# A hybrid decoder block: the output projection by seven products of quarter matrices

## The chip, the cores and the metric

The kernel runs on one core of one Trainium2 chip. The time is the device time of one execution in microseconds (us), taken as the median of several runs. Beside it stands one execution recorded by the hardware profiler. The engines are named as in the profile: PE (TensorE, matrix multiplies; PEld is its weight load), DVE (VectorE), ACT (ScalarE), POOL (GpSimd) and SP (SyncE, which issues most transfers). "SPq" and "POOLq" are the queues in which an engine issues its transfers.

## The reference

One layer on x of 512 tokens by 1024 channels, all in float32. The normalised input goes through one wide projection, whose columns feed two mixers; their results are merged by two gates, and one more projection closes the layer:

```
h = rms_norm(x, norm_pre)
proj = h @ w_in
...
y_a = (o_a * jax.nn.silu(z_n)) @ w_nsa_o
...
y_b = (o_b * jax.nn.silu(z_r)) @ w_ret_o
merged = jax.nn.sigmoid(m_a) * y_a + jax.nn.sigmoid(m_b) * y_b
x = x + rms_norm(merged @ w_out, norm_post)
```

The change is about the last line: `merged @ w_out`, 512 tokens by 1024 channels times 1024 by 1024, its norm over the 1024 outputs of a token, and the sum with x.

## The kernel before, in words

**Precision.** Every float32 operand is split in a high and a low part (`hi` is a rounded copy, made by ACT or DVE; `lo` is the difference, made by DVE in `sub_split`, lines 242 and 209). Each product is three matmuls: high by high, high by low, low by high (`mm3`, line 237; the matmul itself is line 230).

**Order.** All instructions of all engines are put out by one planner at build time (`Order`, line 45). The stages are Python generators that yield what they wait for: a planned time, an engine, or a flag. The planner adds up planned costs for each engine and always continues the generator that could go on first, so the fixed order of each engine's queue comes out of these estimates. At run time the engines wait on semaphores for the data itself.

**Weights.** `stream` (line 1523) lays out all weights in HBM in the order of use, and `stream_shape` names the pieces. SP loads pieces of 128 x 1024 (512 KB) in four raw buffers (`load_next`, line 349; `NR` is 4). `splitter` (line 374) splits each into two weights of 128 x 512 in a ring of nine pairs (`whi`, `wlo`; `NW` is 9). A pair comes free when the matmuls that use it last are put out (`used_up`).

**Seven products.** Two projections, the second halves of the gates `MA` and `MB`, are already done with seven products of quarter matrices in place of eight (`seven`, line 1219; `product`, line 1199; `seven_end`, line 1232). The weight sums that this takes are made in HBM: `weight_sums` (line 328) has POOL issue four copies from DRAM to DRAM tiles and four accumulating transfers for each, while attention runs, and SP later loads the sums like weights. The sums of the other operand are made by DVE (`h_sum`, line 1173). DVE joins the products in `seven_end`.

**The stages in order** (`PLAN`, line 29): `Z`, `MA`, `ZR`, `QK`, `VR` (retention: `ret`, line 1013), then second halves `ZR`, `QK`, `VR`, then `MB`, `NO`, `RO` of the first 512 channels, `MA` by seven, `NO`, `MB` by seven, `RO` of the second. `NO` and `RO` are the projections to `y_a` and `y_b`; their results come channel by channel (four blocks of 128 channels by 512 tokens, `tra`), and `tail_ya` and `tail_yb` (lines 1304, 1311) multiply them with the gates, add them and split the merged block into `MO_H` and `MO_L` (flag `mg0` to `mg7`).

**The last projection before** (end of `main`): two halves of 512 output columns, each for four blocks of 128 tokens, over eight blocks of 128 channels: 2 x 4 x 8 x 3 = 192 matmuls of 512 columns. The last token block of the second half is put out in two pieces of 256 columns. Each weight of 128 x 512 is used by four token blocks, 12 matmuls. `tail_o` (line 1327) handles each block from PSUM: ACT squares it and sums the squares, DVE adds up and multiplies by `norm_post`, POOL takes the power, DVE scales and adds x, and SP stores. `end_loads` (line 1149) loads x and `norm_post` for it.

**In retention**, `ret` has POOL take one power per token block (`rv`, line 1087); the rest of that block's chain on DVE, PE and ACT waits for it.

Of the kernel before, what the change touches and what calls it, by code (L numbers as in the profile page):

```python
# [18 lines left out]
P = 128  # L19
# [120 lines left out]
def block_kernel(ctx: ExitStack, tc, x, xT, x0s, ws, small, w2s, norm_post, rope_r, dmask, out):  # L140
# [101 lines left out]
    def sub_split(lo, src, hi, r, e="dve"):  # L242
        return tt(lo, src, f(hi), OP.subtract, r, e)
# [67 lines left out]


    loads, off = [], 0
    sums, atts = [], [0]
    mark = sp.tile([P, 1], FT, name="mark")
    for pieces in stream_shape():
        if pieces == "seven":
            b11, b12, b21, b22 = (ws[off + i * P * 1024:off + (i + 1) * P * 1024].rearrange("(p n) -> p n", p=P)
                                  for i in range(4))
            t1, t2, t3, t4 = (dp.tile([P, 1040], FT, name=f"t{len(sums)}{i}")[:, 0:1024] for i in range(4))  # L320
            sums.append(((t1, b11), (t3, b12), (t2, b11), (t4, b21), (t1, b12), (t3, b22), (t2, t3), (t4, t2)))
            loads.extend((a, [1024]) for a in (b11, b21, t2, t3, t1, t4, b22))
# [51 lines left out]
    def splitter():  # L374
        for i, (_, pieces) in enumerate(loads):
            n = sum(pieces)
            for k in range(2):
                p = 2 * i + k
                own = KD <= p < 2 * KD
# [9 lines left out]
                if own:  # L389
# [12 lines left out]
                yield  # L402
# [610 lines left out]
    def ret(hp, t, ps, e):  # L1013
# [134 lines left out]

    def end_loads():
        t = bp.tile([P, 28 * 256], FT, name="ends", tag="low")  # L1150
        XR.extend(t[:, o * 256:o * 256 + D] for o in (0, 4, 24, 0))
        OT.extend([*(t[:, o * 256:o * 256 + D] for o in (8, 12, 16)), at(28, D)])
        XR.append(t[:, 20 * 256:20 * 256 + D])
        for t in range(2):
            DMA.dma_start(XR[t], x[t * P:(t + 1) * P, :])
        DMA.dma_start(XR[2], x[2 * P:3 * P, :])
        DMA.dma_start(XR[4], norm_post.rearrange("(o n) -> o n", o=1).broadcast_to([P, D]))

    shr = [0.0] * 4

    def h_sums():
# [70 lines left out]
    def seven_end(st, n, ps, e):  # L1232
# [3 lines left out]
        if n == 0:  # L1236
# [12 lines left out]
        r = max(e, st["ur"])  # L1249

        def gate_of(i, j, b, r):
            sg = sgw[st["off"] // 4].rearrange("p (f c) -> p f c", f=4)[:, 2 * j:2 * j + 2, i * 256:(i + 1) * 256]
            return sg, tt(sg, v, b.rearrange("p (m c) -> p m c", m=2), OP.add, r)
        sg = None
        if n == 1:
            sg, e = gate_of(0, 0, u, r)
# [20 lines left out]
            return  # L1277
        i, j = at_
        yield e, "dve"
        rv = rsrow[:, i * 256:(i + 1) * 256].unsqueeze(1).broadcast_to([P, 2, 256])  # L1280
        e = stt(sg, sg, -1.0, rv, OP.mult, OP.mult, e) if j else tt(sg, sg, rv, OP.mult, e)
        yield e, "act"
        e = act(sg, sg, AF.Tanh, r=e, scale=0.5)
# [20 lines left out]
    def tail_ya(half, ft, ps, e):  # L1304
        yield od.need(f"sg{half}{ft}")
        yield max(e, sgr[ft]), "dve"
        e = stt(sgs[ft], sgs[ft], 1.0, ps, OP.add, OP.mult, e)
        ACC.put(ps, e)
        od.flags.add(f"ya{half}{ft}")

    def tail_yb(half, ft, ps, e):
        yield od.need(f"ya{half}{ft}", f"sg{half}{4 + ft}")
        yield max(e, sgr[4 + ft]), "dve"
        e = stt(sgs[4 + ft], sgs[4 + ft], 1.0, ps, OP.add, OP.mult, e)
        ACC.put(ps, e)
        e = tt(sgs[ft], sgs[ft], sgs[4 + ft], OP.add, e)
        yield e, "act"
        k = half * 4 + ft
        e = act(MO_H[k], sgs[ft], r=e)
        yield e, "dve"  # L1320
        mor[k] = sub_split(MO_L[k], sgs[ft], MO_H[k], e)
        od.flags.add(f"mg{k}")

    mor = [0.0] * 8
    ss2 = cp.tile([P, NT, 3], FT, name="ss2")

    def tail_o(t, i, c0, n, ps, e):

        hc = slice(c0, c0 + n)
        end = c0 + n == D  # L1330
        sq = yield from NAT.get()
        yield e, "act"
        ea = act(sq[:, :n], ps[:, :n], AF.Square, r=e, scale=1.0 / 32.0, accum_out=ss2[:, t, i:i + 1])
        NAT.put(sq, ea)
        yield ea, "dve"
        if i:
            e = ts(ss2[:, t, i:i + 1], ss2[:, t, i:i + 1], ss2[:, t, i - 1:i], 4e-6 if i == 1 else 0.0,
                   OP.add, OP.add, ea)
        if end:
            r2 = sp.tile([P, 1], FT, name="rr", tag="rr", bufs=4)  # L1340
            er = tt(r2, ss2[:, t, i:i + 1], nhalf[:, 0:1], OP.pow, e, "pool")
        e = tt(OT[t][:, hc], ps[:, :n], XR[4][:, hc], OP.mult, ea)
        ACC.put(ps, e)
# [41 lines left out]
    def main():  # L1385
# [126 lines left out]
def stream_shape():  # L1512

    yield [512, 512]
    yield from [[1024]] * 3
    yield from [[560]] * 4
    yield from [[1024]] * (4 + 8)
    for b in PLAN:
        yield from ["seven"] if b in SEVEN else [[1024]] * (2 if b[0] == "NO" else 4)
    yield from [[1024]] * 8  # L1520


def stream(a):
# [22 lines left out]
    for name, i in PLAN:  # L1546
# [41 lines left out]
```

## Time and profile before

| | us |
|---|---|
| median of the runs | 527.37 (527.1 to 527.5) |
| profiled execution, its own time | 526.86 |
| its span, first to last instruction | 525.1 |
| DVE busy | 404.8 |
| ACT busy | 291.9 |
| POOL busy | 25.9 |
| DMA traffic | 68.87 MB, mean 131 GB/s |

The profiled execution's own time is 1.76 us above its span, and the median of the runs 0.5 us above that. Views used below: the page (busy time of each engine), the chain of waits that ended last, tables of stretches of the span (for each engine its busy time, the number of instructions in brackets, then the granted clock of TensorE, the busy share of the DMA engines and GB/s), timelines of one engine (start, duration, engine, line, what it writes and reads, count, and in brackets the idle time before it), and groups of equal instructions. Consecutive matmuls overlap in these records, so the pace is read from start to start.

### The profile page before, as it was taken

How to read it: one execution, taken by the hardware profiler on the slowest of the kernel's cores; microseconds unless marked ns; L12 is line 12 of the kernel's file. 1: busy time of each engine (PE TensorE's matmuls, PEld its weight loads, DVE VectorE, ACT ScalarE, POOL GpSimd, SP SyncE). 2: the span in 40 equal slices, each digit the busy share in tenths (PEclk: the TensorE clock that was granted, in tenths of full speed). 3: DMA queues.
4: the chain of work that ended last, by engine and by line, in shares of the span. 5: the costliest groups of instructions: out<-in, count | busy, mean ns of one | idle time of the engine just before them, and what ended most of it. 6: DMA issues, size and time to landing. Idle time of an engine off the chain costs nothing.

```text
span 525.1 us, 7867 instructions
## 1 busy us (share of the span) xinstructions
PE 514.8 (98%) x2778; PEld 441.3 (84%) x2778; DVE 404.8 (77%) x980; ACT 291.9 (56%) x630; POOL 25.9 (5%) x56
## 2 busy tenths in 40 slices
PE   9999999999999999999999999999999999999995
PEld 7898888788888888888888888888788989988884
DVE  6798799989979799996876576787889867645533
ACT  6663799768568798763515253524557434323411
POOL 1000000000112011000000000000000000000000
PEclk9999999999999999999999999999999999999998
DMA  8941026501667338433131341131644726624032
GB/s 319 392 166 41 21 81 218 183 2 40 213 230 171 111 70 206 126 121 100 42 120 41 140 138 64 42 121 40 220 141 124 238 81 207 208 108 160 2 109 92
DMA packets 22456, 68.87 MB, mean 131 GB/s; under 512 B 2448, under 2 KB 3728, under 8 KB 22416
## 3 DMA queue, kind: packets, MB, share of 16 engines
q1 hardware_dynamic: 19968, 59.84, 32.8%
q0 software_dynamic: 2304, 8.39, 6.9%
q8 instruction: 22, 0.36, 0.3%
q14 instruction: 18, 0.15, 0.1%
q10 hardware_dynamic: 144, 0.14, 0.1%
HBM read 66.26 MB, written 10.49 MB: 146 GB/s over the span
## 4 chain that ended last, share of the span: by engine, by line
PE 81%; DVE 8%; DMA 5%; issue 2%; ACT 1%; SPq 1%; POOL 0%; POOLq 0%; DVEq 0%; ACTq 0%
PE bank L230 76%; PE bank L234 6%; DVE wlo L209 3%; DMA raw<-in_stream_dram 2%; DMA arena_l<-in_x_dram 2%; DVE arena_r L209 1%; DMA arena_l<-in_xT_dram 1%; DMA arena_f<-in_xT_dram 1%; DVE arena_l L846 1%; ACT arena_l L197 1%; DVE arena_l L218 1%; DVE arena_f L209 1%; SPq L479 0%; DVE nat L209 0%; SPq L356 0%
## 5 line engine op out<-in xcount | busy, mean ns | idle before, releaser
L209 DVE TENSOR_TENSOR wlo<-raw,whi 128x512 fp32r<-128x512 f32 x172 | 112.0, 687 | 6.8 <-ACT whi L197 5.7
L197 ACT ACTIVATE whi<-raw 128x512 fp32r<-128x512 f32 x157 | 94.5, 627 | 40.5 <-PE bank L230 33.5
L230 PE MATMUL bank<-whi,hTh 128*128 128x512 f32 x256 | 100.3, 407 | 0.6 <-DVE arena_r L222 0.5
L230 PE MATMUL bank<-whi,hTl 128*128 128x512 f32 x256 | 96.2, 391 | 0.0
L230 PE MATMUL bank<-wlo,hTh 128*128 128x512 f32 x256 | 96.1, 390 | 0.0
L230 PE MATMUL bank<-arena_r 128*128 128x256 f32 (+2 forms) x328 | 70.9, 336 | 0.3 <-DVE arena_r L209 0.3
L230 PE MATMUL bank<-arena_r,whi 128*128 128x512 f32 (+1 forms) x208 | 63.8, 382 | 1.0 <-DVE sg L222 1.0
L197 ACT ACTIVATE arena_l<-arena_l,stat 128x384 f32<-128x384 f32 (+3 forms) x109 | 57.8, 552 | 4.6 <-DVE stat L209 2.5
L197 ACT ACTIVATE arena_r<-bank 128x512 fp32r<-128x512 f32 (+2 forms) x80 | 45.1, 571 | 23.1 <-PE bank L234 21.5
L230 PEld LDWEIGHTS bank<-whi,hTl 128*128 128x128 f32 x256 | 48.1, 188 | 10.7
L230 PEld LDWEIGHTS bank<-whi,hTh 128*128 128x128 f32 x256 | 48.6, 190 | 9.7 <-DVE arena_r L222 0.9
L230 PEld LDWEIGHTS bank<-arena_r 128*128 128x128 f32 x328 | 51.1, 189 | 6.5 <-DVE arena_r L209 0.6
L209 DVE TENSOR_TENSOR arena_r<-bank,arena_r 128x512 fp32r<-128x512 f32 (+2 forms) x72 | 47.1, 657 | 10.9 <-ACT arena_r L197 10.4
L230 PEld LDWEIGHTS bank<-wlo,hTh 128*128 128x128 f32 x256 | 48.3, 188 | 8.2
L230 PE MATMUL bank<-hTh,whi 128*128 128x512 f32 (+1 forms) x144 | 52.4, 364 | 0.0
L230 PE MATMUL bank<-hTh,wlo 128*128 128x512 f32 (+1 forms) x144 | 51.2, 356 | 0.0
L230 PE MATMUL bank<-hTl,whi 128*128 128x512 f32 (+1 forms) x144 | 51.1, 355 | 0.0
L230 PE MATMUL bank<-whi,arena_r 128*128 128x512 f32 (+1 forms) x176 | 48.6, 352 | 0.0
L230 PEld LDWEIGHTS bank<-arena_r,whi 128*128 128x128 f32 x208 | 38.8, 188 | 8.8 <-DVE sg L222 1.6
L230 PE MATMUL bank<-arena_r,wlo 128*128 128x512 f32 x96 | 37.4, 389 | 0.0
L230 PEld LDWEIGHTS bank<-whi,arena_r 128*128 128x128 f32 x176 | 32.2, 189 | 4.6
L234 PE MATMUL bank<-ident,arena_l 128*128 128x128 f32 (+1 forms) x232 | 33.9, 273 | 0.9 <-DVE arena_l L566 0.9
(165 smaller groups left out, 771.0 us busy)
## 6 DMA issues: line engine op xcount, KB each, us to landing
raw<-in_stream_dram SPq DMA_DIRECT2D x77, 512.0 KB, 4.2
t<-in_stream_dram POOLq DMA_DIRECT2D x12, 512.0 KB, 5.4
raw<-t SPq DMA_DIRECT2D x8, 512.0 KB, 3.7
arena_f<-in_rope_r_dram SPq DMA_DIRECT2D x8, 256.0 KB, 2.6
t<-t POOLq DMA_DIRECT2D x4, 512.0 KB, 5.2
arena_f<-in_xT_dram SPq DMA_DIRECT2D x8, 256.0 KB, 3.7
ends<-in_x_dram SPq DMA_DIRECT2D x4, 512.0 KB, 5.4
arena_l<-in_xT_dram SPq DMA_DIRECT2D x7, 256.0 KB, 5.5
```

The lines of the kernel that those rows point to most:

```text
L197: S.activation(o, i, func, **kw)
L209: (V if e == "dve" else G).tensor_tensor(o, a, b, op=op)
L218: V.tensor_scalar(o, a, s1, s2, op0=op0, op1=op1)
L230: T.matmul(ps, a, b, start=start, stop=stop)
L234: T.transpose(ps, a, idn)
L846: V.tensor_tensor_reduce(pv[:, b, :], sv[:, b, :], maskp[:, 512 - L:512], 1.0, -NEG, OP.add, OP.min, nm[:, b:b + 1])
```

## The change

The last projection is cut in quarters: tokens 0 to 255 and 256 to 511, channels in two halves, output columns in two halves. With merged quarters a (token half, channel half) and weight quarters b (channel half, column half), it takes seven products, each of two blocks of 128 tokens by four blocks of 128 channels by 512 columns.

- **Weights.** `stream` gives four quarters of two pieces each. The four weight sums, of two pieces each, are made by 16 transfers that POOL issues (`out_sums`): eight copies to DRAM tiles, then eight accumulating ones. Three follow the power of each of the first four token blocks in `ret`, and one that of each of the second four (`OSUMS`). SP loads 14 pieces in place of eight. The last eight weights have places of their own, which come free after the second `RO`.
- **Merged sums.** `s_early` makes the sum that needs the first channel half only, `s_late` the three others, on DVE, with splits by ACT and DVE into the places of `hTh` and `hTl`. The gates of the second half go to new places (`G1`), so that the first merged half stays.
- **Products.** `out_seven` runs seven products into PSUM banks `X` (products 1, 3, 5, 7), `Q` (2, 4) and `Y` (6). Where a product's partial value is needed in another sum, ACT copies the bank first (`keep`) and the next product adds to it in PSUM. The last product finishes its first token block before its second.
- **Tails.** `tail_o` takes a kept copy to add (`plus`) for six of eight blocks. Its final scaling is in three pieces for token block 1; the second piece of block 0 is put behind the power of block 1. x comes in two loads with `norm_post` after the gates, and two after the merged sums.

```
+        if pieces == "out":
+            b11, b12, b21, b22 = ([ws[off + i * P * 1024:off + (i + 1) * P * 1024].rearrange("(p n) -> p n", p=P)
+                                   for i in range(2 * q, 2 * q + 2)] for q in range(4))
+            t1, t2, t3, t4 = ([dp.tile([P, 1040], FT, name=f"o{i}{j}")[:, 0:1024] for j in range(2)] for i in range(4))
+            for a, b in ((t1, b11), (t3, b12), (t2, b11), (t4, b21), (t1, b12), (t3, b22), (t2, t3), (t4, t2)):
+                osums.extend(zip(a, b))
+            loads.extend((a, [1024]) for q in (b11, t3, t2, t4, t1, b21, b22) for a in q)
...
+    def out_sums(n):
...
+        for _ in range(n):
+            i = len(oissued)
+            o, a = osums[i]
+            if i < 8:
+                G.dma_start(o, a)
+            else:
+                G.dma_start(o, a, accum_op=OP.add)
+            od.op("pool", 900.0)
+            oissued.append(i)
...
+        out_sums(OSUMS[4 * hp + t])
...
+    def s_early(s):
...
+        yield od.need("end00", "end01", "end10", "end11")
+        t = yield from RS.get()
+        yield 0.0, "dve"
+        e = tt(t, sgs[s][:, 0:256], sgs[s][:, 256:512], OP.subtract)
+        yield e, "act"
+        sor[0][s] = yield from s_split(2 * s + 1, slice(0, 256), t, e)
+        RS.put(t, sor[0][s])
+        od.flags.add(f"se{s}")
...
+    def s_late(s, r):
+        yield r, "dve"
+        m0, m1, t = sgs[s], G1[s], sgs[4 + s]
+        e = tt(t[:, 0:256], m1[:, 256:512], m0[:, 256:512], OP.subtract, r)
+        e = stt(t[:, 256:512], t[:, 0:256], -1.0, m0[:, 0:256], OP.mult, OP.subtract, e)
+        es = e
+        yield e, "act"
+        sor[1][s] = yield from s_split(2 * s, slice(0, 512), t, e)
+        od.flags.add(f"sl{s}")
+        yield 0.0, "act"
+        mor[4 + s] = yield from mo_split(4 + s, m1, 512, r)
+        yield od.need(f"se{s}")
+        yield es, "dve"
+        e = stt(m0[:, 256:512], t[:, 256:512], -1.0, m1[:, 0:256], OP.mult, OP.subtract, es)
+        yield e, "act"
+        s4r[s] = e = yield from s_split(2 * s + 1, slice(256, 512), m0[:, 256:512], e)
+        od.flags.add(f"s4{s}")
+        if all(f"s4{i}" in od.flags for i in range(4)):
...
+    def tail_o(t, i, ps, e, plus=None):
+        hc = slice(i * 512, (i + 1) * 512)
+        o = OT[t][:, hc]
+        if plus:
+            yield lambda: len(plus[0]) > plus[1]
+            b, r = plus[0][plus[1]]
+            yield max(e, r), "dve"
+            e = tt(o, ps, b, OP.add, max(e, r))
+            free[t, i] = e
+            src = o
+        else:
+            src = ps
+        yield e, "act"
+        ea = act(rsrow, src, AF.Square, r=e, scale=1.0 / 32.0, accum_out=ss2[:, t, i:i + 1])
...
+            e = ts(ss2[:, t, 1:2], ss2[:, t, 1:2], ss2[:, t, 0:1], 4e-6, OP.add, OP.add, ea)
...
+            er = tt(r2, ss2[:, t, 1:2], nhalf[:, 0:1], OP.pow, e, "pool")
+            od.flags.add(f"pow{t}")
+        tt(o, src, XR[4][:, hc], OP.mult, ea)
+        if not i:
             return
...
+        if t > 1:
+            yield lambda: len(parts) == 2 * len(loads)
+        for a, b in ((0, 512), (512, D)) if t != 1 else ((0, 384), (384, 768), (768, D)):
+            if t == 0 and a:
+                yield od.need("pow1")
             e = stt(OT[t][:, a:b], OT[t][:, a:b], r2, XR[t][:, a:b], OP.mult, OP.add, e)
             DMA.dma_start(out[t * P:(t + 1) * P, a:b], OT[t][:, a:b])
...
+        plan = ((X, quarter(0, 0)), (Q, summed(2)), (X, summed(1)), (Q, quarter(1, 1)), (X, summed(0)),
+                (Y, quarter(0, 1)), (X, summed(3)))
+        first, last = (0, 1, 5), (3, 5, 6)
+        for n, (ps, (of, src)) in enumerate(plan):
...
+            for ms in ((0, 1),) if n < 6 else ((0,), (1,)):
+                for s in range(4):
+                    name, rd, k = src(s)
+                    yield od.need(name)
+                    yield rd[k] + PE_LAG
+                    yield blk.ready(4 * n + s)
+                    yield blk.ready(4 * n + s)
+                    wh, wl, r = blk.views(4 * n + s)
+                    for m in ms:
+                        lh, ll = of(s, m)
+                        for i, (a, b) in enumerate(((lh, wh), (ll, wh), (lh, wl))):
+                            T.matmul(ps[m], a, b, start=n in first and s + i == 0, stop=n in last and s + i == 5,
+                                     skip_group_check=True)
+                            e = od.pe(228.2, r)
+                    if ms[-1] == 1:
+                        used_up(e)
+                if n == 6:
+                    od.spawn(tail_o(ms[0], 1, ps[ms[0]], e), 1)
+            for m in range(2):
+                if n == 0:
+                    if m == 0:
+                        od.spawn(flip(), 1)
+                    od.spawn(keep(ps[m], p1, e), 1)
+                elif n == 1:
+                    od.spawn(keep(ps[m], p7, e), 1)
+                elif n == 2:
+                    od.spawn(keep(ps[m], u1, e, G1[2 + m]), 1)
+                elif n == 3:
+                    od.spawn(tail_o(2 + m, 0, ps[m], e, (u1, m)), 1)
+                elif n == 4:
+                    od.spawn(tail_o(2 + m, 1, ps[m], e, (p7, m)), 1)
+                elif n == 5:
+                    od.spawn(tail_o(m, 0, ps[m], e, (p1, m)), 1)
+
...
-        for half in range(2):
-            blk = Block(8, 512)
-            for t in range(NT):
-                c = slice(t * P, (t + 1) * P)
-                n = 256 if half and t == NT - 1 else 512
-                for j in range(512 // n):
-                    ps, e = yield from nat(blk, t, n, t == NT - 1 and (j + 1) * n == 512,
-                                           lambda kt: MO_H[kt][:, c], lambda kt: MO_L[kt][:, c], j * n, merged)
-                    od.spawn(tail_o(t, half + j, half * 512 + j * n, n, ps, e), 1)
...
+        od.flags.add("gb")
+        yield from out_seven()
```

More of the change, by code (lines that the diff above doesn't have):

```diff
@@ L40 @@
 HOLD = 1500.0
+OSUMS = (3, 3, 3, 3, 1, 1, 1, 1)
 CAPS = (0, 4, 8, 11, 14, 16, 16, 16, 16)
@@ L302, in block_kernel @@
     XH = Ring([at(o, 512) for o in (28, 38, 40)])
+    G1 = []
     SH, low = [], [arena_l]
@@ L313, in block_kernel @@
     loads, off = [], 0
-    sums, atts = [], [0]
+    sums, osums, oissued, atts = [], [], [], [0]
     mark = sp.tile([P, 1], FT, name="mark")
@@ L378, in splitter @@
                 p = 2 * i + k
-                own = KD <= p < 2 * KD
+                late = p - 2 * len(loads) + 8
+                own = KD <= p < 2 * KD or late >= 0
+                if late >= 0:
+                    yield od.need("gb")
                 yield lambda: own or in_ring(p) < in_ring(len(done)) + NW
@@ L388, in splitter @@
                 src = raws[i][0][:, k * m:(k + 1) * m]
-                if own:
+                if late >= 0:
+                    hi, lo = at(4 * late, 512, FR), at(4 * late + 2, 512, FR)
+                elif own:
                     hi, lo = WC[p - KD]
@@ L1150, in end_loads @@
         t = bp.tile([P, 28 * 256], FT, name="ends", tag="low")
[L1151 to L1154, printed above, removed]
+        v = [t[:, o * 256:o * 256 + D] for o in range(0, 28, 4)]
+        OT.extend(v[0:4])
+        XR.extend([at(30, D), at(34, D), *v[4:7]])
+        DMA.dma_start(XR[4], norm_post.rearrange("(o n) -> o n", o=1).broadcast_to([P, D]))
+        for t in range(2, 4):
             DMA.dma_start(XR[t], x[t * P:(t + 1) * P, :])
-        DMA.dma_start(XR[2], x[2 * P:3 * P, :])
-        DMA.dma_start(XR[4], norm_post.rearrange("(o n) -> o n", o=1).broadcast_to([P, D]))
+            od.dma(P * 4096)
     shr = [0.0] * 4
@@ L1243, in seven_end @@
         yield od.need(*[f"mg{k}" for k in range(4)])
+        if not st["off"]:
+            yield od.need("sh3")
         if n == 3:
@@ L1251, in gate_of @@
         def gate_of(i, j, b, r):
-            sg = sgw[st["off"] // 4].rearrange("p (f c) -> p f c", f=4)[:, 2 * j:2 * j + 2, i * 256:(i + 1) * 256]
-            return sg, tt(sg, v, b.rearrange("p (m c) -> p m c", m=2), OP.add, r)
+            c = slice(i * 256, (i + 1) * 256)
+            bv = b.rearrange("p (m c) -> p m c", m=2)
+            if st["off"]:
+                sg = [(sgw[1].rearrange("p (f c) -> p f c", f=4)[:, 2 * j:2 * j + 2, c], v, bv)]
+            elif j:
+                sg = [(at(38, 1024).rearrange("p (f c) -> p f c", f=2)[:, :, c], v, bv)]
+            else:
+                sg = [(G1[m][:, c].unsqueeze(1), v[:, m:m + 1, :], bv[:, m:m + 1, :]) for m in range(2)]
+            for g, a, b in sg:
+                r = tt(g, a, b, OP.add, r)
+            return [g for g, _, _ in sg], r
         sg = None
@@ L1279, in seven_end @@
         yield e, "dve"
-        rv = rsrow[:, i * 256:(i + 1) * 256].unsqueeze(1).broadcast_to([P, 2, 256])
-        e = stt(sg, sg, -1.0, rv, OP.mult, OP.mult, e) if j else tt(sg, sg, rv, OP.mult, e)
+        for g in sg:
+            rv = rsrow[:, i * 256:(i + 1) * 256].unsqueeze(1).broadcast_to([P, g.shape[1], 256])
+            e = stt(g, g, -1.0, rv, OP.mult, OP.mult, e) if j else tt(g, g, rv, OP.mult, e)
+        if st["off"]:
+            od.flags.add(f"end{i}{j}")
         yield e, "act"
-        e = act(sg, sg, AF.Tanh, r=e, scale=0.5)
+        for g in sg:
+            e = act(g, g, AF.Tanh, r=e, scale=0.5)
         for m in range(2):
@@ L1306, in tail_ya @@
         yield max(e, sgr[ft]), "dve"
-        e = stt(sgs[ft], sgs[ft], 1.0, ps, OP.add, OP.mult, e)
+        a = (sgs, G1)[half][ft]
+        e = stt(a, a, 1.0, ps, OP.add, OP.mult, e)
         ACC.put(ps, e)
@@ L1315, in tail_yb @@
         ACC.put(ps, e)
-        e = tt(sgs[ft], sgs[ft], sgs[4 + ft], OP.add, e)
-        yield e, "act"
-        k = half * 4 + ft
-        e = act(MO_H[k], sgs[ft], r=e)
+        a = (sgs, G1)[half][ft]
+        e = tt(a, a, sgs[4 + ft], OP.add, e)
+        if half:
+            od.spawn(s_late(ft, e), 1)
+            return
+        yield e, "act"
+        mor[ft] = yield from mo_split(ft, a, 256, e)
+        od.spawn(s_early(ft), 1)
+    RS = Ring([rsrow[:, 0:256], rsrow[:, 256:512]])
+    sor = [[0.0] * 4 for _ in range(2)]
@@ L1320, in tail_yb, with mo_split @@
+    def mo_split(k, a, n, r):
+        e = act(MO_H[k][:, 0:n], a[:, 0:n], r=r)
         yield e, "dve"
-        mor[k] = sub_split(MO_L[k], sgs[ft], MO_H[k], e)
+        e = sub_split(MO_L[k][:, 0:n], a[:, 0:n], MO_H[k][:, 0:n], e)
         od.flags.add(f"mg{k}")
-    mor = [0.0] * 8
[L1325 to L1331, printed above, removed]
-        yield e, "act"
-        ea = act(sq[:, :n], ps[:, :n], AF.Square, r=e, scale=1.0 / 32.0, accum_out=ss2[:, t, i:i + 1])
-        NAT.put(sq, ea)
+        return e
@@ new lines, in s_split @@
+    def s_split(i, c, a, r):
+        e = act(hTh[:, i, c], a, r=r)
+        yield e, "dve"
+        return sub_split(hTl[:, i, c], a, hTh[:, i, c], e)
+    def s_early(s):
[7 more added lines that the diff above has]
+        od.flags.add(f"se{s}")
@@ new lines, in s_late @@
+    def s_late(s, r):
[16 more added lines that the diff above has]
+        if all(f"s4{i}" in od.flags for i in range(4)):
+            for t in range(2):
+                DMA.dma_start(at(30 + 4 * t, D), x[t * P:(t + 1) * P, :])
+                od.dma(P * 4096, max(s4r))
@@ new lines, in block_kernel, with keep @@
+    s4r = [0.0] * 4
+    mor = [0.0] * 8
+    G1.extend([maskp, at(28, 512), at(38, 512), at(40, 512)])
+    ss2 = cp.tile([P, NT, 2], FT, name="ss2")
+    p1, p7 = [], []
+    def keep(ps, lst, e, dst=None):
+        if dst is None:
+            dst = yield from NAT.get()
+        else:
+            yield od.need("s42", "s43")
+        yield e, "act"
+        e = act(dst, ps, r=e)
+        lst.append((dst, e))
+    def tail_o(t, i, ps, e, plus=None):
[8 more added lines that the diff above has]
+            src = o
+        else:
+            src = ps
+        yield e, "act"
+        ea = act(rsrow, src, AF.Square, r=e, scale=1.0 / 32.0, accum_out=ss2[:, t, i:i + 1])
@@ L1351, in tail_o, with out_seven, quarter, of @@
+        for a, b in ((0, 512), (512, D)) if t != 1 else ((0, 384), (384, 768), (768, D)):
+            if t == 0 and a:
+                yield od.need("pow1")
             e = stt(OT[t][:, a:b], OT[t][:, a:b], r2, XR[t][:, a:b], OP.mult, OP.add, e)
             DMA.dma_start(out[t * P:(t + 1) * P, a:b], OT[t][:, a:b])
-        if t == 0:
-            DMA.dma_start(XR[3], x[3 * P:4 * P, :])
-            od.flags.add("xr3")
+    free = {}
+    def out_seven():
+        blk = Block(28, 512)
+        X = [(yield from PS.get()), (yield from PS.get())]
+        Q = [(yield from PS.get()), (yield from PS.get())]
+        Y, u1 = [], []
+        def quarter(i, j):
+            def of(s, m):
+                c = slice(i * 256 + m * P, i * 256 + (m + 1) * P)
+                return MO_H[4 * j + s][:, c], MO_L[4 * j + s][:, c]
+            return of, lambda s: (f"mg{4 * j + s}", mor, 4 * j + s)
+        def summed(w):
+            def of(s, m):
+                c = slice(w % 2 * 256 + m * P, w % 2 * 256 + (m + 1) * P)
+                return hTh[:, 2 * s + w // 2, c], hTl[:, 2 * s + w // 2, c]
+            return of, lambda s: (f"sl{s}", sor[1], s) if w < 2 else (f"se{s}", sor[0], s) if w == 2 else (f"s4{s}", s4r, s)
+        plan = ((X, quarter(0, 0)), (Q, summed(2)), (X, summed(1)), (Q, quarter(1, 1)), (X, summed(0)),
+                (Y, quarter(0, 1)), (X, summed(3)))
+        first, last = (0, 1, 5), (3, 5, 6)
+        for n, (ps, (of, src)) in enumerate(plan):
+            if n == 5:
+                for _ in range(2):
+                    Y.append((yield from ACC.get()))
+            if n in (2, 3, 4, 6):
+                if n == 6:
+                    yield lambda: all((2 + m, 1) in free for m in range(2))
+                    r = max(free[2, 1], free[3, 1])
+                else:
+                    lst = {2: p1, 3: p7, 4: u1}[n]
+                    yield lambda: len(lst) == 2
+                    r = max(e for _, e in lst)
+                yield r + PE_LAG
+            for ms in ((0, 1),) if n < 6 else ((0,), (1,)):
[14 more added lines that the diff above has]
+                        used_up(e)
+                if n == 6:
+                    od.spawn(tail_o(ms[0], 1, ps[ms[0]], e), 1)
[14 more added lines that the diff above has]
+                    od.spawn(tail_o(m, 0, ps[m], e, (p1, m)), 1)
@@ L1358, in masks, with flip @@
+    def flip():
+        yield 0.0, "act"
+        act(XR[4][:, 512:D], XR[4][:, 512:D], scale=-1.0)
     def masks():
@@ L1519, in stream_shape @@
         yield from ["seven"] if b in SEVEN else [[1024]] * (2 if b[0] == "NO" else 4)
-    yield from [[1024]] * 8
+    yield "out"
 def stream(a):
@@ L1551, in stream @@
         out += block(name, i)
-    for half in range(2):
-        out += pair(w_out[:, half * 512:(half + 1) * 512])
+    out += [a for r in range(2) for c in range(2) for a in pair(w_out[r * 512:(r + 1) * 512, c * 512:(c + 1) * 512])]
     return np.concatenate([o.reshape(-1) for o in out])
```

14 lines of the change are left out of this document (1 added, 13 removed).

## The prediction

> **What bounds the kernel now.** First the page: how much of the span is PE at work?
>
> ```profile
> span 525.1 us, 7867 instructions
> ## 1 busy us (share of the span) xinstructions
> PE 514.8 (98%) x2778; PEld 441.3 (84%) x2778; DVE 404.8 (77%) x980; ACT 291.9 (56%) x630; POOL 25.9 (5%) x56
> ```
>
> 98% alone does not say that a shorter PE shortens the kernel, since matmul records overlap. So next the chain that ended last, in order of time. Its last PE piece:
>
> ```profile
> 377.22 136.65 PE bank L230 x763
> 514.19 0.54 POOL rr L209
> ```
>
> For 136 us nothing but PE decides. Then a table of stretches, for the last projection (first two rows), the second `RO` without and with its last pass, and `MB` by seven, the nearest stretch to what the change builds.
>
> ```profile
> core 0: us, PE busy (x) PEld busy (x) DVE busy (x) ACT busy (x) POOL busy (x), PEclk, DMA share, GB/s
> 474.84:513.03 38.19, 38.19 (x170) 31.65 (x169) 15.94 (x26) 9.81 (x21) 1.10 (x2) 1.00 0.25 83
> 513.03:518.83 5.80, 5.80 (x49) 5.60 (x47) 2.77 (x6) 1.16 (x4) 0.54 (x1) 1.00 0.25 91
> 453.08:469.40 16.32, 16.32 (x75) 13.50 (x73) 6.64 (x10) 2.54 (x4) 0.00 (x0) 1.00 0.54 194
> 469.40:474.84 5.44, 5.44 (x26) 4.51 (x24) 5.11 (x9) 4.21 (x7) 0.00 (x0) 1.00 0.25 96
> 433.00:453.00 20.00, 20.00 (x169) 20.00 (x168) 16.02 (x25) 10.20 (x17) 0.00 (x0) 1.00 0.56 185
> ```
>
> The reader is to see PE without a gap at granted clock 1.00 in every row, while DVE and ACT have room in the last projection (15.94 and 9.81 of 38.19 us) but little in the pass before (5.11 of 5.44). **PE bounds this stage**, so each matmul removed counts in full until another engine fills up.
>
> **The change part by part. Matmuls.** Seven token blocks of 8 x 3 matmuls with 512 columns, 168, and then two half-wide pieces, 48 with 256 columns, stand in the code before. The timeline of PE gives the cut:
>
> ```profile
> 474.84 0.39 PE L230 MATMUL bank<-whi,arena_r 128*128 128x512 f32 x1
> ...
> 513.03 0.28 PE L230 MATMUL bank<-wlo,arena_r 128*128 128x256 f32 x1
> ```
>
> So 168 matmuls take 38.19 us, 0.2273 each. The change issues 7 products x 4 channel blocks x 2 token blocks x 3 = 168 of the same shape, again with merged blocks stationary and weights moving. If PE waits for nothing, its last one is issued where the first 256-wide one was, at 513.03, and the stretch behind it, **5.80 us**, goes.
>
> **The tail.** From the timeline of DVE:
>
> ```profile
> 513.90 0.21 DVE L218 TENSOR_SCALAR ss<-ss 128x1 f32<-128x1 f32 x1 [3.14 <-ACT nat L197]
> 514.03 0.68 DVE L209 TENSOR_TENSOR ends<-bank,ends 128x512 f32<-128x512 f32 x1
> 514.77 1.42 DVE L222 SCALAR_TENSOR_TENSOR ends<-ends,rr 128x512 f32<-128x512 f32 x2
> ...
> 520.30 1.54 DVE L222 SCALAR_TENSOR_TENSOR arena_f<-arena_f,rr,ends 128x384 f32<-128x384 f32 x3 [0.33 <-POOL rr L209]
> ```
>
> The token block that ends at 513.03 has a 512-wide tail, exactly what the new last block has: its first scaling starts at 514.77, 1.74 us after the last issue. Today's last block is 256 wide and needs 520.30 - 518.83 = 1.47. That costs 0.27. One thing more: the second scaling of token block 0 is held until the power of block 1 is out, and is put between block 1's multiply and its scalings: 1.42 / 2 = 0.71 us. It can hide only in the gap before the power returns, about 0.06 us (multiply ends at 514.71). So block 1 scales from about 515.4, needs the same 1.54 us in three pieces, and ends at 517.0. From there to the end of the span I keep today's 525.1 - 521.84 = 3.26 us, plus 0.1 for block 0's 256 KB just ahead in the queue. End: 520.3. **Sum: -5.80 + 0.27 + 0.65 + 0.1 = -4.8 us.**
>
> **DVE and ACT in the stage.** Durations by group:
>
> ```profile
> L209 DVE TENSOR_TENSOR wlo<-raw,whi 128x512 fp32r<-128x512 f32 x37 | 24.6, 688 | 2.5 <-ACT whi L197 2.3
> L222 DVE SCALAR_TENSOR_TENSOR ends<-ends,rr 128x512 f32<-128x512 f32 x6 | 4.2, 750 | 0.2
> ...
> L218 DVE TENSOR_SCALAR ss<-ss 128x1 f32<-128x1 f32 x5 | 1.1, 214 | 13.8 <-ACT nat L197 13.8
> L205 DVE CAST whi<-raw 128x512 fp32r<-128x512 f32 x2 | 0.8, 424 | 0.0
> L209 DVE TENSOR_TENSOR arena_f<-bank,ends 128x256 f32<-128x256 f32 x2 | 0.8, 414 | 0.0
> ```
>
> From 469.40, when the ring of weights comes free, to 513.03 (43.6 us) DVE has: 27 of 28 `lo` parts (one fits before), 18.6; three `hi` copies, 1.3; `tail_yb` and `s_late` of the last two channel blocks, each four 512-wide (2.75) and four 256-wide operations (1.7), 8.9; in the tails six adds and seven multiplies at 0.69, five scalings at 0.75 and three small ones, 13.3. Together **42.1 of 43.6 us** at recorded durations. But these overlap when DVE runs on without a wait:
>
> ```profile
> 472.66 3.10 DVE L209 TENSOR_TENSOR wlo<-raw,whi 128x512 fp32r<-128x512 f32 x5
> ```
>
> Five in 3.10 us: 0.60 each, not 0.69. At that pace the 42.1 are about 37. So the cover holds at either end, by 1.5 to 6.6 us; gone, each us too much would be a us on the end. I take 37, the pace of a DVE that has work queued, hence nothing for PE. In the order it is needed it also fits: by 485.7, two products in, PE has used eight weights, and DVE needs 7.8 (merged blocks) + 9 x 0.6 = 13.2 of 16.3 us.
>
> ACT has hi copies, keeps, splits and squares: 24 + 6 + 4 + 7 of 512 and two of 256, about 41 x 0.63 + 0.8 = 27 of 43.6 us, by this row:
>
> ```profile
> L197 ACT ACTIVATE whi<-raw 128x512 fp32r<-128x512 f32 x157 | 94.5, 627 | 40.5 <-PE bank L230 33.5
> ```
>
> `s_early` (four times two 256-wide operations, 3.3 us) and the first two `s_late` (2.4 us each beyond what is there) fall in 453 to 469, where DVE is busy 6.64 of 16.32: nothing. The waits between products are covered by a product in between: `keep` reads `X` after product 1, and product 3 writes it 24 x 0.2273 = 5.45 us later; two copies take 1.3. Product 7 waits for two adds on DVE behind product 5, again with 5.45 us between. Before the second `RO` the gates of `MA` need two more half-wide passes for each of two quarters, 4 x (2 x 0.41 - 0.69) = 0.5 us of DVE, and the first merged half's narrower low parts give back 4 x 0.27: nothing. What each queued wait would block: on SP, raw loads behind the two late x loads (wait for the last `s_late`); four raws ahead, 8 x 1.36 = 11 us of PE, cover it.
>
> **Loads.** Six more raws of 512 KB:
>
> ```profile
> raw<-in_stream_dram SPq DMA_DIRECT2D x77, 512.0 KB, 4.2
> t<-in_stream_dram POOLq DMA_DIRECT2D x12, 512.0 KB, 5.4
> ```
>
> A raw lands in 4.2 us and is split in about 2 x 0.63 + 0.69 + some waiting, 2.5; with four buffers one comes every 6.7 / 4 = 1.7 us, and PE needs one per 12 x 0.2273 = 2.73. Nothing, up to a landing of 4 x 2.73 - 2.5 = 8.4 us.
>
> **Weight sums on POOL.** The 16 transfers stand behind a power in `ret`, in front of the next one. POOL's own timeline shows the like for `MA` and `MB`, and those powers:
>
> ```profile
> 139.50 1.80 POOL L336 DMA_DIRECT2D t<-in_stream_dram  x3
> ...
> 158.28 0.84 POOL L338 DMA_DIRECT2D t<-in_stream_dram  x1 [0.40 <-issue]
> 163.95 0.84 POOL L338 DMA_DIRECT2D t<-in_stream_dram  x1 [4.82 <-issue]
> ...
> 247.66 0.73 POOL L209 TENSOR_TENSOR rv<-rv,nhalf 128x2 f32<-128x2 f32 x1 [12.48 <-DVE rv L216]
> 257.10 0.69 POOL L209 TENSOR_TENSOR rv<-rv,nhalf 128x2 f32<-128x2 f32 x1 [8.72 <-DVE rv L216]
> 271.99 1.00 POOL L209 TENSOR_TENSOR rv<-rv,nhalf 128x2 f32<-128x2 f32 x1 [14.20 <-DVE rv L216]
> 283.30 0.70 POOL L209 TENSOR_TENSOR rv<-rv,nhalf 128x2 f32<-128x2 f32 x1 [10.30 <-DVE rv L216]
> 325.70 0.70 POOL L209 TENSOR_TENSOR rv<-rv,nhalf 128x2 f32<-128x2 f32 x1 [41.70 <-DVE rv L216]
> ```
>
> Three copies go out in 1.80 us; accumulating ones follow each other by 5.67 (158.28 to 163.95), about one landing. Behind 247.66 and 257.10 POOL is held 1.8 us of 9.4 and 14.9; behind 271.99 two copies and one accumulating, at most 1.8 + 5.4 of 11.3; behind 283.30 three accumulating, up to 17 us of 42.4. No power is late: nothing on the path. If each transfer held POOL for a landing, it would be 3 x 5.4 = 16 us in a gap of 9.4.
>
> **The rivals.**
>
> - *Small waits* (chance 0.20): weights or sums come late by 1 to 3 us in all, as DVE stands at its upper price, 42.1 of 43.6, with ACT results to wait for. 523.5 to 525.5. For it: DVE is full in 469.40 to 474.84. Against: PE had no gap there.
> - *DVE becomes the bound, slower* (0.08). Place: 469.40 to 513.03. DVE's queue is in order, and each `lo` part, split and tail operation waits for ACT in it. If DVE reaches a busy share s, the stage takes 42.1 / s. At s = 0.87 that is 48.4 us, 4.8 over, and the gain is gone: from there on it is slower. At 0.80, the share in 433.00 to 453.00, it is 52.6: +9.0 - 4.8, 531.5. Against: there PE, not DVE, set the pace, and 5.11 of 5.44 is 0.94.
> - *POOL holds the retention powers* (0.04). At a landing for each copy the powers of blocks 2 to 4 come up to 2.6, 4 and 10 us late (three landings against gaps of 9.4, 14.9 and 11.3, carried on), and PE, in order, waits for the transposes behind them: up to +10 - 4.8, 532.5. Against: three copies in 1.80 us. [...]
> - *A little more gain* (0.10): block 0's scaling finds its gap, or one of the existing short waits of PE goes with the new order: 521.0 to 521.8.
>
> That PE does not get shorter at all can be left out: the number of matmuls is fixed by the code.
>
> **How the numbers follow.** The sum is against the profiled execution: span 525.1 - 4.8 = 520.3, own time 526.86 - 4.8 = 522.1. The median of the runs is 0.5 higher, so 527.37 - 4.8 = 522.6; I say **522.5**, with 521.9 to 523.4 for this case (chance 0.58). The range 521.3 to 525.5 takes in the small waits and most of the extra gain and leaves out the two bad cases. A measurement of this kernel tells about 0.2%, 1.05 us, from no change. Faster by more than that (below 526.3): 0.58 + 0.20 + 0.10 = 0.88, less 0.01 for small waits that grow, 0.87; within: 0.04; slower: 0.09.
>
> **What would show it.** Right: 168 matmuls of 512 columns in about 38.2 us, none of 256 in the last stage, no idle PE in front of any of the seven products, and 7.3 us from the last issue to the end, with a 512-wide scaling between block 1's multiply and its own. Wrong: PE idle released by DVE `lo` parts or `arena_r` splits (small waits, or DVE as the bound), by a raw load (landing over 8.4 us), or at 257 to 300 by what follows a power that starts after a transfer. If the last issue is at 513.0 and the time still differs, the tail was mis-sized.

## The result and the profile after

| | before, us | after, us |
|---|---|---|
| median of the runs | 527.24 | 522.02 (521.49 to 522.43) |
| span of the profiled execution | 525.1 | 519.7 |
| first matmul of the last projection | 474.84 | 474.69 |
| last matmul of it, end of its issue | 518.83 | 512.77 |
| from there to the end of the span | 6.27 | 6.93 |

The ratio is 0.9902 (95% interval 0.9885 to 0.9919), 5.2 us less; forecast were 4.8 less, 522.5. The span is shorter by 5.4: 0.15 at the start of the stage, 43.99 - 38.08 = 5.91 in its matmuls, and 0.66 given back in the tail.

The busy line of the page after:

```profile
span 519.7 us, 7889 instructions
## 1 busy us (share of the span) xinstructions
PE 509.3 (98%) x2730; PEld 435.4 (84%) x2730; DVE 426.7 (82%) x1033; ACT 304.0 (58%) x656; POOL 38.0 (7%) x72
```

And the table of stretches: last pass of the second `RO`, the seven products, the tail, and the first two together.

```profile
core 0: us, PE busy (x) PEld busy (x) DVE busy (x) ACT busy (x) POOL busy (x), PEclk, DMA share, GB/s
469.25:474.69 5.44, 5.44 (x26) 4.51 (x25) 5.25 (x10) 4.70 (x9) 0.00 (x0) 1.00 0.30 97
474.69:512.77 38.08, 38.08 (x169) 31.36 (x167) 32.99 (x61) 19.91 (x42) 2.41 (x3) 1.00 0.52 180
512.77:519.70 6.93, 0.16 (x1) 0.00 (x0) 3.51 (x7) 0.69 (x2) 0.54 (x1) 0.88 0.42 151
469.25:512.77 43.52, 43.52 (x193) 35.87 (x191) 38.24 (x70) 24.61 (x50) 2.41 (x3) 1.00 0.49 169
```

PE has no gap in its 38.08 us, as forecast. But the DVE column has gone from 15.94 to 32.99 us in the same length. The chain that ended last still names PE up to its last matmul:

```profile
377.07 97.78 PE bank L231 x588
474.85 38.09 PE bank L1513 x168
513.02 0.60 ACT rsrow L198
513.88 0.68 DVE ends L210
514.56 0.66 DVE ends L223
515.22 0.53 DVEq L1756
515.75 0.92 DVE ends L223 x2
```

Read with DVE's timeline, the same tail looks closer:

```profile
512.61 0.75 DVE L223 SCALAR_TENSOR_TENSOR ends<-ends,rr,arena_f 128x512 f32<-128x512 f32 x1
513.75 0.21 DVE L219 TENSOR_SCALAR ss<-ss 128x1 f32<-128x1 f32 x1 [0.39 <-ACT rsrow L198]
513.88 0.68 DVE L210 TENSOR_TENSOR ends<-bank,ends 128x512 f32<-128x512 f32 x1
514.47 2.20 DVE L223 SCALAR_TENSOR_TENSOR ends<-ends,rr,arena_f 128x512 f32<-128x512 f32 x4
```

When block 1's sum of squares arrives, at 513.75, DVE has been free for 0.39 us only. A chain names one path and does not say how near the next is. DVE's queue is a second path, 0.39 us behind. The four scalings in 2.20 us begin with the held one of block 0, the rest is block 1's.

### The profile page after: what moved, and what is told of

The parts are those of the page before. It is cut to its first block, busy times and chain, and to the rows that moved or that the text cites. A ratio compares the mean times of both kernels' runs of the same rounds, so it can differ in the third digit from the quotient of the medians.

```text
span 519.7 us, 7889 instructions
## 1 busy us (share of the span) xinstructions
PE 509.3 (98%) x2730; PEld 435.4 (84%) x2730; DVE 426.7 (82%) x1033; ACT 304.0 (58%) x656; POOL 38.0 (7%) x72
## 4 chain that ended last, share of the span: by engine, by line
PE 82%; DVE 9%; DMA 5%; ACT 1%; issue 1%; SPq 0%; DVEq 0%; ACTq 0%
PE bank L231 69%; PE bank L1513 7%; PE bank L235 6%; DMA raw<-in_stream_dram 5%; DVE wlo L210 3%; DVE arena_r L210 1%; DVE arena_l L873 1%; DMA arena_f<-in_xT_dram 1%; DVE arena_l L219 1%; DVE arena_f L210 1%; DVE nat L210 0%; ACT arena_l L198 0%; ACT whi L198 0%; DVE whi L206 0%; DVE ends L223 0%
## 5 line engine op out<-in xcount | busy, mean ns | idle before, releaser
L210 DVE TENSOR_TENSOR wlo<-raw,whi 128x512 fp32r<-128x512 f32 x176 | 114.8, 686 | 9.7 <-ACT whi L198 8.7
L235 PEld LDWEIGHTS bank<-ident,arena_l 128*128 128x128 f32 (+1 forms) x232 | 27.9, 138 | 6.8 <-DVE arena_l L593 1.1
L873 DVE CUSTOM_DVE_ANT_0 arena_l<-bank,maskp 128x512 f32<-128x512 f32 (+3 forms) x64 | 29.3, 486 | 3.0 <-PE bank L231 2.7
```

What stands on the lines that cost most here:

```text
L210: (V if e == "dve" else G).tensor_tensor(o, a, b, op=op)
L235: T.transpose(ps, a, idn)
L873: V.tensor_tensor_reduce(pv[:, b, :], sv[:, b, :], maskp[:, 512 - L:512], 1.0, -NEG, OP.add, OP.min, nm[:, b:b + 1])
```

## The experiments

In all of them the stage is measured inside the profile, from the first matmul of the last projection to the end of the span, in the two parts of the table above. This leaves out what happened earlier: in the profiles of kernels that are the same up to there, the stage begins between 474.51 (E11) and 476.28 us (E3; more in the last section). The changed kernel has 38.08 + 6.93 = 45.01 us. Ratios are to the kernel before, with 95% intervals.

**More and less PE.**

```
 T.matmul(ps[m], a, b, start=n in first and s + i == 0, stop=n in last and s + i == 5,
          skip_group_check=True)
+if n == 4:
+    T.matmul(ps[m], a, b, start=False, stop=False, skip_group_check=True)
```

> The changed kernel (522.0 us, span 519.7), with the 24 matmuls of product 5 put out twice; the value doubles that product. Theory (PE alone sets the last stage): 24 x 0.2273 = 5.45 us more, 527.5. Rival (DVE's queue sets it, PE has hidden room): less than 3 us more, under 525.

E1 measured: 527.27 (ratio 1.0012, 1.0003 to 1.0021), stage 43.52 + 6.94 = 50.46, 5.45 more. More PE costs its full price.

```
+if i == 1 and n < 2:
+    e = od.pe(228.2, r)
+    continue
 T.matmul(ps[m], a, b, start=n in first and s + i == 0, stop=n in last and s + i == 5,
          skip_group_check=True)
```

> The changed kernel without the low-by-high matmuls of products 1 and 2: 16 matmuls fewer, all other work the same. Theory (PE sets the stage, DVE delivers the ninth weight 2.7 us ahead of its use, as the trace after shows): 16 x 0.2273 = 3.64 us less PE, of which 2.7 are gained, 519.3. PE alone, with DVE far ahead: 518.4. DVE as dear as its recorded durations (room 1.5 us): 520.5.

E2 measured: 521.91 (ratio 0.9909, 0.9894 to 0.9923): nothing gained. Its two parts:

```profile
475.71:510.89 35.18, 34.76 (x153) 28.27 (x151) 30.36 (x56) 17.73 (x37) 1.87 (x2) 1.00 0.54 189
510.89:520.40 9.51, 0.15 (x1) 0.00 (x0) 5.92 (x12) 2.45 (x8) 1.08 (x2) 0.72 0.37 132
```

PE does end 2.9 us earlier, with one wait of 0.42, but the tail grows from 6.93 to 9.51, and in it DVE is busy 5.92 us instead of 3.51. All three expectations were off: PE alone, the room by recorded durations, and the spare time at the ninth weight, which looks only at what PE waits for. The whole stage is 44.69, 0.3 shorter. The chain that ended last names no PE in this stage. It runs over DVE, one raw load and DVE again:

```profile
486.01 2.50 DVE wlo L210 x4
488.52 7.51 DMA raw<-in_stream_dram
496.48 0.86 DVE arena_r L210 x2
```

So the second path is DVE's queue together with a raw load that it waits for.

With the same matmuls left out of all seven products (`if i == 1:`):

> The same for all seven products: 56 matmuls fewer, 12.7 us of PE. PE alone: 509.3. Theory (DVE becomes the bound: by the trace after it is busy 38 to 39 us of the 43.6 from 469 to 512.8): about 5 us less, 517, with PE idle in front of weights. DVE at the forecast's upper price, 42.1 us: 520.5.

E3 measured: 521.6 (ratio 0.991, 0.9883 to 0.9936), stage 44.32: 0.7 of 12.7 us. PE is no longer the bound, as the theory had it, but there was almost no room in place of 5 us. The chain that ended last runs over DVE and two raw loads, 6.35 us from 486.69 and 5.35 from 495.40: the bound is DVE's queue with its loads, not DVE's work alone. Here PE waits:

```profile
504.08 6.65 PE L1516 MATMUL bank<-arena_r,hTh 128*128 128x512 f32 x16 [3.44 <-DVE ends L210]
```

Product 7 stands 3.44 us in front of the adds of product 5, which DVE takes late.

**More DVE.** In `s_late`, for the third and fourth channel block, the low part is made again `k` times, 2 or 6:

```
 sor[1][s] = yield from s_split(2 * s, slice(0, 512), t, e)
+for _ in range(k if s > 1 else 0):
+    V.tensor_tensor(hTl[:, 2 * s, 0:512], t, f(hTh[:, 2 * s, 0:512]), op=OP.subtract)
```

> The changed kernel with four low parts of the merged sums made again by DVE (two each for the third and the fourth channel block), 4 x 0.60 = 2.4 us more DVE ahead of the ninth weight. Theory (the ninth weight has 2.7 us to spare): no change, 522.0 within 0.5. Room of 1.5 us (recorded durations): about 1 us more, 523.0.

E4 measured: 524.92 (ratio 0.9962, 0.995 to 0.9974), 2.9 us more; stage 47.68, 2.67 more.

```profile
475.32:513.42 38.10, 38.10 (x169) 31.31 (x167) 32.92 (x60) 17.57 (x37) 1.87 (x2) 1.00 0.48 173
513.42:523.00 9.58, 0.16 (x1) 0.00 (x0) 6.05 (x12) 2.59 (x8) 1.08 (x2) 0.77 0.38 137
```

PE does not wait at all (38.10 again). The added parts hold DVE's queue for 1.34 and 1.33 us, 2.67 together, from 475.58 and 483.18 on, both over 28 us before the last matmul; all of it comes out behind that matmul. So it was right that the ninth weight had time to spare, and wrong that this spare time was the stage's. DVE's later waits do not take the work up either. In front of the cast for which DVE waits 1.93 us in the changed kernel (shown under "The raw loads") it now waits longer:

```profile
496.01 0.43 DVE L206 CAST whi<-raw 128x512 fp32r<-128x512 f32 x1 [2.82 <-DMA raw<-o]
```

A raw is loaded into a buffer that a `lo` part of DVE has freed: between 475 and 500 us SP's queue waits for DVE's `wlo` seven times in the changed kernel, 14.4 us in all, and 17.1 us here. A later DVE makes a later load.

> The same with twelve low parts made again, 7.2 us more DVE at the same place. Theory (it is the place that counts: 2.7 us to spare at the ninth weight): 4.5 us more, 526.5, with PE idle in front of product 3 and DVE idle later in the stage. Room counted over the whole stage at the queued pace (6.6 us): 0.6 us more, 522.6. Over the whole stage at recorded durations (room 1.5): 12 x 0.69 - 1.5 = 6.8 more, 528.8.

E5 measured: 530.72 (ratio 1.0064, 1.0044 to 1.0085), stage 53.50, 8.49 more: dearer than any of the three prices, the recorded durations' 6.8 included, and slower than the kernel before. The twelve parts hold DVE's queue for 8.48 us (474.87 to 479.11 and 485.37 to 489.61), not the 7.2 expected, and again all of it is paid. Now PE waits too, in product 3:

```profile
491.62 0.80 PE L1515 MATMUL bank<-wlo,hTh 128*128 128x512 f32 x1 [4.75 <-DVE wlo L210]
```

That is the 4.5 us theory's wait, at its place and nearly of its size, but it is not the price: DVE's queue up to the end is.

**Less DVE, alone and with less PE.** These form the test of two tied paths. The multiplies by `norm_post` of token blocks 2 and 3 are left out, first with E2's shorter PE, then alone:

```
-tt(o, src, XR[4][:, hc], OP.mult, ea)
+if t > 1:
+    od.op("dve", 602.0, ea, True)
+else:
+    tt(o, src, XR[4][:, hc], OP.mult, ea)
```

> The kernel without the low-by-high matmuls of products 1 and 2, and without the four multiplies by norm_post of token blocks 2 and 3 (4 x 0.60 us of DVE after the weights are split). New theory (DVE's queue runs from the raw's arrival to the end): 2.4 us less, stage 42.4, 519.5. Rival (something else than DVE's queue took the place of PE): no change.

> The changed kernel (stage 45.0, 522.0) without the same four multiplies. New theory (PE ends last there, DVE only 0.4 us behind): 0 to 0.4 us less, 521.6 to 522.0. If DVE's queue alone bound the changed kernel: 2.4 less, 519.6.

E10 and E11 measured: 520.1 for both together (ratio 0.9866, 0.9845 to 0.9887), stage 35.18 + 7.63 = 42.81; 521.56 for the multiplies alone (ratio 0.9894, 0.9874 to 0.9915), stage 38.08 + 6.91 = 44.99. The parts of E10 (first two rows) and of E11:

```profile
475.09:510.27 35.18, 34.74 (x153) 28.26 (x151) 29.50 (x54) 19.46 (x42) 1.12 (x2) 1.00 0.55 195
510.27:517.90 7.63, 0.16 (x1) 0.00 (x0) 4.50 (x10) 0.79 (x4) 1.08 (x2) 0.83 0.38 137
474.51:512.59 38.08, 38.08 (x169) 31.34 (x167) 31.29 (x57) 19.97 (x42) 1.66 (x3) 1.00 0.51 180
512.59:519.50 6.91, 0.16 (x1) 0.00 (x0) 2.92 (x6) 0.69 (x2) 0.54 (x1) 0.88 0.42 152
```

Less PE alone brought 0.3 us, less DVE alone nothing, both together 2.2. What either path gains alone the other keeps; **PE and DVE's queue end within half a us of each other** in the changed kernel.

**The raw loads.** In the changed kernel DVE is not full all the time. Its timeline, where it waits longest:

```profile
488.58 1.29 DVE L210 TENSOR_TENSOR wlo<-raw,whi 128x512 fp32r<-128x512 f32 x2 [0.97 <-ACT whi L198]
491.80 0.43 DVE L206 CAST whi<-raw 128x512 fp32r<-128x512 f32 x1 [1.93 <-DMA raw<-o]
```

and the load issues of 470 to 500 us by group (size, median us to landing):

```profile
raw<-o SPq DMA_DIRECT2D x6, 512.0 KB, 4.4
raw<-in_stream_dram SPq DMA_DIRECT2D x4, 512.0 KB, 6.4
arena_f<-in_x_dram SPq DMA_DIRECT2D x2, 512.0 KB, 5.5
```

Is it the x loads in front that keep the raw back? In E2's kernel they were put behind the last raw load:

```
-for t in range(2):
-    DMA.dma_start(at(30 + 4 * t, D), x[t * P:(t + 1) * P, :])
+od.spawn(x_late(), 1)
...
+def x_late():
+    yield lambda: len(raws) == len(loads)
```

> The kernel without the low-by-high matmuls of products 1 and 2 (521.9 us; its last stage, first matmul to the end, about 44.8), with the two late x loads put behind the last raw load. New theory (beside PE runs a second chain of almost the same length: raw loads and DVE's queue; in that kernel DVE idles 2.2 us for a raw that lands behind the x loads): the second chain gets about 2 us shorter, stage 42.9, 520.0. Rival (DVE's amount of work alone is the second chain, and the loads do not matter): no change, 44.8 and 521.9. First theory (PE alone): 3.6 us less than the changed kernel already, which the run without the move did not show.

E9 measured: 522.21 (ratio 0.9907, 0.9884 to 0.9931), stage 45.62, 0.9 longer. DVE's waits are still there:

```profile
490.85 0.69 DVE L210 TENSOR_TENSOR wlo<-raw,whi 128x512 fp32r<-128x512 f32 x1 [1.92 <-ACT whi L198]
...
495.15 0.43 DVE L206 CAST arena_r<-raw 128x512 fp32r<-128x512 f32 x1 [1.36 <-DMA raw<-in_stream_dram]
```

So the x loads in front are not what makes DVE wait for raws. Whether the move alone would shorten the second path is not shown: with it the planner also put two more `hi` copies on DVE and two `lo` parts ahead of the adds of product 4, which can account for the longer stage. No run shortens the raw loads alone, so how the second path divides into DVE's work and the loads' landing stays open.

**The weight sums on POOL.** Transfers left out, and plain quarters loaded:

```
-loads.extend((a, [1024]) for q in (b11, t3, t2, t4, t1, b21, b22) for a in q)
+loads.extend((a, [1024]) for q in (b11, b12, b21, b22, b12, b21, b22) for a in q)
...
 if i < 8:
-    G.dma_start(o, a)
-else:
-    G.dma_start(o, a, accum_op=OP.add)
+    pass
```

> The changed kernel without the 16 transfers on POOL; SP loads the plain weight quarters in the places of the sums. Theory (they stand on no path): 522.0 within 0.5. Rival (POOL's transfers hold the retention powers, or take bandwidth from loads that PE needs): faster by 1 us or more.

E6 measured: 521.7 (ratio 0.9897, 0.9879 to 0.9916), first matmul of the stage at 474.83 against 474.69, stage 44.97 against 45.01. The 16 transfers, 8.4 MB by POOL's queue, cost nothing. POOL's timeline of the changed kernel shows why:

```profile
248.35 0.73 POOL L210 TENSOR_TENSOR rv<-rv,nhalf 128x2 f32<-128x2 f32 x1 [12.51 <-DVE rv L217]
249.06 1.63 POOL L344 DMA_DIRECT2D o<-in_stream_dram  x3
257.78 0.71 POOL L210 TENSOR_TENSOR rv<-rv,nhalf 128x2 f32<-128x2 f32 x1 [7.09 <-DVE rv L217]
...
284.02 0.71 POOL L210 TENSOR_TENSOR rv<-rv,nhalf 128x2 f32<-128x2 f32 x1 [5.36 <-DVE rv L217]
284.70 0.88 POOL L346 DMA_DIRECT2D o<-in_stream_dram  x1
290.19 0.83 POOL L346 DMA_DIRECT2D o<-in_stream_dram  x1 [4.61 <-issue]
298.81 0.82 POOL L346 DMA_DIRECT2D o<-in_stream_dram  x1 [7.79 <-issue]
326.42 0.71 POOL L210 TENSOR_TENSOR rv<-rv,nhalf 128x2 f32<-128x2 f32 x1 [26.80 <-DVE rv L217]
```

Each power still waits for DVE, not for POOL. The three accumulating transfers take 15 us of the gap of 42. The copies' issues take 0.54 us each, those for `MA` and `MB` 0.55 (means of eight).

**The tail.** First without the hold of block 0's second scaling:

```
-if t == 0 and a:
-    yield od.need("pow1")
```

> The changed kernel without the wait of token block 0's second scaling for the power of block 1. Theory: it runs at 513.3 to 514.05, puts block 1's small addition off by 0.3 us and frees 0.66 behind it: the tail from the last matmul's issue to the end goes from 6.9 to 6.6 us, 521.7. Rival (the hold is worth what it costs): tail 6.9 or more.

E7 measured: 522.33 (ratio 0.9901, 0.9882 to 0.9919), stage 38.08 + 6.91: no gain. Its DVE timeline:

```profile
514.07 1.41 DVE L223 SCALAR_TENSOR_TENSOR ends<-ends,rr,arena_f 128x512 f32<-128x512 f32 x2
515.40 0.21 DVE L219 TENSOR_SCALAR ss<-ss 128x1 f32<-128x1 f32 x1
515.52 0.68 DVE L210 TENSOR_TENSOR ends<-bank,ends 128x512 f32<-128x512 f32 x1
```

The addition at 515.40 has no idle time in front: PE's last issue ended at 513.79, and what took 0.98 us from there to the addition now takes 1.61. What the scaling no longer costs behind, it costs in front. Then, on top of that edit, with the two scalings of block 3 behind the adds of product 6:

```
+if (0, 0) in free and (1, 0) in free:
+    od.flags.add("yadd")
...
+if t == 3:
+    yield od.need("yadd")
```

> As the one before, and the two scalings of token block 3 put behind the adds of product 6. DVE now takes these adds 1.0 us after product 6 ends, since it is in the scalings; ACT's squares, and with them block 0's tail, come that much later. Theory: block 0 is done before block 1's addition at 513.75, the whole 0.66 goes: tail 6.3, 521.4. Rival (DVE is full from 507 to 514, so what is moved comes back): tail 6.6 or more.

E8 measured: 521.51 (ratio 0.989, 0.987 to 0.991), stage 38.08 + 6.32 = 44.40. The tail is shorter by 0.61, as expected (0.66).

```profile
512.81 1.41 DVE L223 SCALAR_TENSOR_TENSOR ends<-ends,rr,arena_f 128x512 f32<-128x512 f32 x2
514.66 0.21 DVE L219 TENSOR_SCALAR ss<-ss 128x1 f32<-128x1 f32 x1 [0.43 <-ACT rsrow L198]
```

Block 0 is done 0.43 us before block 1's addition. The same with the x loads put late, as in E9:

> The changed kernel with the scalings of token block 3 behind the adds of product 6 and no hold for block 0 (521.5, stage 44.4), and the two late x loads behind the last raw load. New theory: PE is the bound and the tail behind it has its shortest form already, so the shorter second chain brings nothing more in a quiet run: stage 44.3, 521.4. If the second chain still held the tail back: stage 43.7 or less, 520.8.

E12 measured: 521.51 (ratio 0.9893, 0.9874 to 0.9912), stage 38.08 + 6.42 = 44.50. The move gains nothing. These two are the shortest stages with the whole computation. By their times they can't be told from the changed kernel (522.02); the profiles' tails show the 0.5 to 0.6 us.

## Why the prediction was right, and where it was not

- **Matmuls.** Right: 168 in 38.08 us where 38.19 were read from the trace of before, no gap, and the stretch of 5.80 gone. One product more costs 5.45 us (E1).
- **Tail.** The place was right, the hold included (0.66 us between block 1's multiply and its scalings); the size was 7.27 against 6.93. The term that was too large is what follows DVE's last scaling: I kept 3.26 + 0.1, and it took 519.7 - 516.67 = 3.03.
- **POOL.** Right, and the rival with it fell: nothing is late, the copies' issues took 0.54 us each, and without the transfers nothing is gained (E6). One sum of this rival does not come out of its rows: three landings of 5.4 us against gaps of 9.4, 14.9 and 11.3, carried on, make the powers 6.8, 8.1 and 13.0 us late, not 2.6, 4 and 10, and the time 535.6 instead of 532.5.
- **DVE's cover.** This is the step that was mis-sized. I took 37 us of work in 43.6 and read the difference, 6.6, as room. The work came out near it, 38.24 of 43.52 (with five `hi` copies where three were counted). But the 5.3 us of idle time are not room. Of them 3.6 lie before 495 us, nearly all in waits for ACT and for raws, and 1.7 behind 503, in waits of at most 0.47 for ACT's sums and POOL's powers. What comes later can't be moved into them, and work put in ahead of them is not taken up, as the raws then come later too (E4). Room at the end was 0.39 us by the trace. The forecast's sentence that "each us too much would be a us on the end" is what E4 and E5 show (2.67 for 2.67, 8.49 for 8.48), only that it holds at once and not from 1.5 or 6.6 us on. The rival of DVE as the bound, given 0.08, was half a us from taking over.
- **Loads.** I had nothing up to a landing of 8.4 us. The four last raws took 6.4 (median), and PE did not wait; DVE did, which the step did not ask.

The matmuls and the tail carry the sum, and there the mechanism was right. That nothing had to be added for DVE was luck: it ended 0.39 us before it mattered, where the forecast had read 1.5 to 6.6. Slightly dearer splits or adds would have taken the gain back us for us.

## What to carry to other kernels

Idle time summed over a stage is not room: ask when the queue of the second engine would be empty at the end if the first were infinitely fast, and count only idle time that the added work can be moved into. A wait for a load that the same engine starts, by freeing its buffer, moves along with the engine's queue (here the wait of 1.93 us became 2.82, behind 2.67 us of added work, E4). When a change shortens the bound and fills another engine, test it from both sides, a little more and a little less on each: full price for more on either and nothing for less on either is the mark of two tied paths. Work on such a stage has to shorten both at once.

## What the runs showed of the hardware

- **The clock of a waiting PE.** In E3, behind the 3.44 us in which PE waited, the 16 matmuls of product 7 take 6.65 us, about 0.41 each where they take 0.227 otherwise. The table of stretches of that run shows the granted clock there:

```profile
495.00:500.00 5.00, 4.65 (x20) 3.41 (x19) 5.00 (x10) 2.51 (x5) 0.00 (x0) 1.00 0.49 161
500.00:505.00 5.00, 1.56 (x5) 1.02 (x4) 4.43 (x9) 2.70 (x7) 0.00 (x0) 0.81 0.00 1
505.00:510.00 5.00, 5.00 (x13) 3.86 (x12) 4.09 (x9) 0.51 (x2) 1.87 (x2) 0.50 0.28 105
```

  From 505 to 510 us it is 0.50, half. Where it falls is an estimate from means of the granted clock, taking one step from 1.00 to 0.50. In E3, in the wait of 3.44 us, the mean of 0.81 from 500 to 505 us puts it at about 503.1, 2.5 us after PE's last matmul (500.64). In E5, where PE waits 4.75 us from 486.87 on, the mean is 0.96 both from 475 to 515 and from 474.60 to 520.01 us, which is 3.2 and 3.6 us at half, and the matmuls are back at their pace at about 494.9 (the record of 494.77 is 0.45 us long, the next 0.39): the fall is at about 491.5, 4.6 us after PE's last matmul. In E3 it cost nothing, as PE was not on the chain that ended last.
- **A wait far ahead of the change.** Profiled executions differ by up to 1.8 us before the last stage begins. For 0.9 us of it the place is seen. The chains of the changed kernel and of the E8 kernel, which share all code up to there, are within 0.1 us of each other from 105 us on until a load of xT for the sums of `MA`:

```profile
369.49 3.94 DMA arena_f<-in_xT_dram
```

```profile
370.01 4.99 DMA arena_f<-in_xT_dram
```

  With the longer landing PE waits 0.99 us at 377 and the stage begins at 475.60, with the shorter one it begins at 474.69. E3, at 476.28, is 1.2 us late already at 107 us. That this is also what parts the changed kernel's four times, 521.49 and 521.65 from 522.39 and 522.43, is likely but not shown.
- **Accumulating transfers.** Three in a row follow each other on POOL by 5.5 and 8.6 us (284.70, 290.19, 298.81), although they write different tiles and the copies before them go out at 0.54 us each.
